# A hybrid encoder step on one core: the order of the first stage, the identity, the PSUM banks of the long projections, and the rank of attention

## The chip, the cores and the metric

The kernel is one program on one core of a Trainium2 chip. It is written in a language in which the author names every instruction and its engine. A scheduler at compile time then fixes the order in which each engine works its instructions off, and puts in the semaphores. The metric is the device time of one execution in microseconds (us). Two executions of the same program differ a little, so a time is given as the median of several runs.

The engines are TensorE (PE, matrix products, with a separate row PEld for the loading of weights), VectorE (DVE), ScalarE (ACT), GpSimd (POOL) and SyncE (SP), whose only work here is to issue transfers.

## The reference

One layer of a streaming encoder works on 384 tokens: 256 of a new stream and 8 running streams of 16 tokens each. All data are float32. With D = 2048:

```python
h    = rmsnorm(x, norm_mix_g)
proj = h @ w_in            # columns: GLU in (2048), q, k, v (1024 each), forget logits (8), gates A and B (2048 each)
u    = glu_in[..., :1024] * sigmoid(glu_in[..., 1024:])
z    = layernorm(causal_dwconv(ext(u), conv_dw_w, conv_dw_b))        # 31 taps
a    = (z * sigmoid(z)) @ conv_pw_out
q, k = rmsnorm(q), rmsnorm(k)
b    = forgetting_attention(q, k, v, logf, caches) @ w_att_out        # 8 heads of 128
x    = x + (sigmoid(gA) * a + sigmoid(gB) * b) @ w_out
h2   = rmsnorm(x, norm_ffn_g)
g, v = split(h2 @ w_up)                                               # 5632 each
x    = x + (silu(causal_dwconv(ext(g), ffn_dw_w, ffn_dw_b)) * v) @ w_down   # 3 taps
```

Beside x the new keys, values, log forget gates and convolution states are returned.

## The kernel before

**Products in three passes.** Each float32 operand of a large product is split into a high part `hi`, in the engine's rounded format, and a low part `lo`, the rest. A product is then three matmuls: hi·hi, lo·hi and hi·lo. Weights come from memory as a stream of tiles `raw`, one per pair of 128-row blocks. The list `plan` holds all 480 pairs in the order of their use. `fetch` (L132) issues the load on SP, `split` (L148) makes `hi` by a copy on ACT (L145) and `lo` by a subtraction on DVE (L146). There are three buffers each for `raw`, `hi` and `lo`. `ahead(n)` (L199) keeps two or three pairs split in advance; its loads and splits carry a priority raised by `SPLIT_AHEAD` = 150.

**Rows of work.** `gemm` (L221) walks a list of jobs. A job of kind "B" has the 384 tokens as three row tiles of up to 512 columns, so it holds three PSUM banks; a job of kind "A" (only the GLU columns) holds four. After each block of 128 rows (a unit: 9 matmuls for "B", 12 for "A") `tick` (L212) advances the side work, which is written as generators: `first_norm`, `bias_rows`, `attention`, `conv`, `layer_norm`. At the end of a job its `evac` takes the banks off to SBUF under a priority raised by `EVAC_AHEAD` = 400. PSUM has eight banks: five in the pool `acc` for the jobs, three in the pool `misc` for transposes and small products.

**What sets the order.** All of PE's instructions run in the order of the source (`pe_order`, L291). On the other engines the scheduler picks, of the instructions that its model calls ready, the one of the best rank. Three devices restrict it. The very first block (L293 to L321) is in source order on SP, ACT and DVE. `queued(d)` (L91) ties an instruction behind the last one queued on its engine. `keep_in_program_order` ties an instruction behind the one traced before it on its engine. Neither adds a wait: they only fix the order, and an engine works strictly along it.

**The first stage.** The columns of v are made first, in three jobs of 344 columns; the first two share one walk over the rows, and the weight tiles of the two alternate. During this walk `first_norm` brings in the input: `x_chunk(c)` (L282) transposes three token tiles by PE into a `misc` bank (L285), and ACT and DVE write the parts of `hT` from it (L288, L289). ACT also sums squares of x (L399), and after the last chunk `rsqrt` gives the row factors `rs1` with which v is scaled when it leaves PSUM (`tok_evac`, L423). The loads of the first sixteen weight pairs are chained on SP with the loads of x; their splits, the `x_chunk` evacuations and the other ACT and DVE work are not chained. The identity for the transposes is made by a helper on POOL (a memset and a select); eight small loads follow on POOL (L348 to L352).

**Keys and queries.** `tok_evac` is called with the index `sq` for k and q. For each of the three banks it writes the rows and then, still inside the raised priority, sums the squares of four heads on ACT (L433).

**Attention and convolution** run beside the GLU jobs. `attention` (L651) starts one head every six units, in six steps: `head_past_keys` (the cached keys transposed on DVE, L571, and the load of the next head's cached keys, L574), `head_operands`, `head_scores`, `head_probs`, `head_out`, `head_last`. All of it has the ordinary rank. `conv` (L686) does 31 taps for each of eight channel groups on DVE (L722) at the ordinary rank, and goes on into the gate jobs.

**After it** come the gate jobs (L823), the two projections of a and b (`AO_PW`, L178) with the mixing, `w_out`, and the feed-forward part (`FFN_PLAN`, L170), all of kind "B" with 512 columns.

Of the kernel before, what the change touches and what calls it, by code (L numbers as in the profile page):

```python
# [15 lines left out]
P = 128  # L16
# [17 lines left out]
SPLIT_AHEAD, EVAC_AHEAD = 150, 400  # L34
# [6 lines left out]
def hybrid_step(  # L41
# [102 lines left out]
    def split_rows(hi, lo, raw, o, k):  # L144
        nc.scalar.copy(hi[:, k, :o], raw[:, k, :o])  # L145
        tt(lo[:, k, :o], raw[:, k, :o], f(hi[:, k, :o]), op=ALU.subtract)  # L146
# [44 lines left out]
    v_last = len(plan) - 16  # L191
    ready = []
# [89 lines left out]
    def x_chunk(c):  # L282
        ps = misc_tile()
        for t in range(NTT):
            tr(ps[:, t * P:(t + 1) * P], xs[c // 4][:, t, c % 4 * P:(c % 4 + 1) * P], ident[:])  # L285
        g = gm[:, c:c + 1]
        hi, lo = hT[c // 4][:, 0, c % 4, :], hT[c // 4][:, 1, c % 4, :]
        nc.scalar.activation(hi, ps[:, :NT], AF.Identity, scale=g)  # L288
        stt(lo, ps[:, :NT], g, f(hi), op0=ALU.mult, op1=ALU.subtract)  # L289
# [57 lines left out]
    for v, r, n in rows:  # L347
        nc.gpsimd.dma_start(vrow[r:r + n, :], v[0].rearrange("(c p) -> c p", p=P))  # L348
    kg = p_qkv.tile([P, P], F32, name="kg")
    nc.gpsimd.dma_start(kg[:], k_norm_g[0].partition_broadcast(P))  # L350
    bf = p_qkv.tile([P, H], F32, name="bf")
    nc.gpsimd.dma_start(bf[:], b_forget[0].partition_broadcast(P))  # L352
# [35 lines left out]
    def first_norm():  # L388
        for c in range(2, 16, 2):
            if c == 2:  # L390
                yield
            yield
            x_chunk(c)
            yield
            x_chunk(c + 1)
            if c % 4 == 2:
                for t in range(NTT):
                    n = c // 4
                    tc.keep_in_program_order(  # L399
                        nc.scalar.activation(junk[:], xs[n][:, t, :], AF.Square, accum_out=ssx[:, t, n:n + 1]))  # L400
            yield
            if c > 2:
                yield
        mt = p_x0.tile([P, NTT], F32, name="mt")
        nc.vector.tensor_reduce(mt[:], ssx[:], axis=mybir.AxisListType.X, op=ALU.add)
        ts(mt[:], mt[:], 1.0 / DM, EPS, op0=ALU.mult, op1=ALU.add)
        r = rsqrt(mt[:], [P, NTT], p_x0, "r1")
        nc.vector.tensor_copy(rs1[:], r[:])
        for _ in range(12):
# [13 lines left out]
    def tok_evac(dst, c0, n, sq=None, shared=True):  # L423
        def ev(t, ps):
            if shared and t % 2:
                ts(dst[:, t, c0:c0 + n], ps[:, :n], rs1[:, t:t + 1], None, op0=ALU.mult)
            else:
                nc.scalar.activation(dst[:, t, c0:c0 + n], ps[:, :n], AF.Identity, scale=rs1[:, t:t + 1])
            if sq is not None:
                for i in range(n // P):  # L430
                    jk = p_qkv.tile([P, P], F32, tag="jk", bufs=2, name="jk")
                    h = c0 // P + i
                    nc.scalar.activation(jk[:], dst[:, t, h * P:(h + 1) * P], AF.Square,  # L433
                                         accum_out=ssq[:, sq, t, h:h + 1])
        return ev
# [78 lines left out]
    gemm([job("B", 16, ha, tok_evac(kt, 512 * i, 512, 0)) for i in range(2)], [bias_rows()])  # L514
# [9 lines left out]
    gemm([job("B", 16, ha, tok_evac(qt, 512 * i, 512, 1)) for i in range(2)])  # L524
# [44 lines left out]
    def head_past_keys(d):  # L569
# [3 lines left out]
        if d["h"] + 1 < H:  # L573
            load_k(d["h"] + 1)  # L574
# [76 lines left out]
    def attention():  # L651
# [171 lines left out]
    gemm([job("B", 16, ha, sig_evac(sg, n)) for sg in (sgA, sgB) for n in range(4)], [ln_steps])  # L823
# [10 lines left out]
    gemm([ao_job(n) for _, n in AO_PW[:2]], [ln_steps])  # L834
# [30 lines left out]
    def pw_done(n):  # L865
        def done():
# [8 lines left out]
          for what, n in AO_PW[2:]])  # L875
# [56 lines left out]
    gemm([job("B", 16, grouped(mix), wo_evac(n), done=wo_done(n)) for n in range(4)])  # L932
# [93 lines left out]
    for what, g in FFN_PLAN:  # L1026
        gemm(up_jobs(g) if what == "up" else down_jobs(g, g[-1] == 10))
# [45 lines left out]
```

## Time and profile before

| | us |
|---|---|
| median of 3 runs | 2005.14 (2003.96 to 2006.22) |
| the profiled execution, time | 2005.83 |
| its span, first to last instruction | 2003.9 |
| PE busy (9431 matmuls) | 1992.6 |
| PEld busy | 1681.5 |
| DVE busy | 1272.2 |
| ACT busy | 742.1 |
| POOL busy | 87.2 |
| mean granted PE clock | 0.999 |

The page of the profile gives, for each engine, the time in which it worked on something and its share of the span. Idle time of an engine has a cause: a wait for a semaphore, which the view of the waits names by the instruction that released it. A matmul's recorded length overlaps that of the next, so the distance from start to start tells its cost. The clock that the throttle granted to PE is a share of full speed. The memory moved 137 GB/s on average over the span.

### The profile page before, as it was taken

Reading aid. Unit: us, or ns where it says so; the run is one execution under the profiler, and the core shown is the slowest. Engines: PE = TensorE matmul, PEld = TensorE weight load, DVE = VectorE, ACT = ScalarE, POOL = GpSimd, SP = SyncE. Lnnn points to the kernel's source line nnn. Section 1 sums busy time; section 2 is a strip of 40 time slices with the busy share of each in tenths; the row PEclk is TensorE's granted clock in tenths of the full one; section 3 lists DMA queues with packets and bytes.
Section 4 is the critical chain, followed back from the end, with each engine's and each line's share of the span. In section 5 each row is a group of like instructions: output and inputs, shape, how many; then the busy total and the mean of one; then the engine's idle time right before and its main releaser. Section 6 shows DMA issues by size and latency. Waiting matters only on the chain.

```text
span 2003.9 us, 24493 instructions
## 1 busy us (share of the span) xinstructions
PE 1992.6 (99%) x9431; PEld 1681.5 (84%) x9431; DVE 1272.2 (63%) x1852; ACT 742.1 (37%) x1077; POOL 87.2 (4%) x216
## 2 busy tenths in 40 slices
PE   8999999999999999999999999999999999999999
PEld 8988999988888887888888888888888888888887
DVE  4435478888765487676867683367673376638663
ACT  5434455433334523334433432233332233323321
POOL 2000001100000000000010000001000000000000
PEclk9999999999999999999999999999999999999999
DMA  6566566444444334534444444444443444344443
GB/s 179 176 175 175 137 163 167 120 140 131 132 134 125 127 121 142 185 121 133 127 137 116 137 127 137 126 127 126 129 135 127 133 120 137 126 129 125 137 157 106
DMA packets 209254, 275.99 MB, mean 138 GB/s; under 512 B 55878, under 2 KB 96729, under 8 KB 209129
## 3 DMA queue, kind: packets, MB, share of 16 engines
q1 hardware_dynamic: 208817, 273.85, 46.3%
q8 instruction: 74, 1.21, 0.2%
q0 software_dynamic: 288, 0.57, 0.2%
q14 instruction: 43, 0.35, 0.1%
q10 hardware_dynamic: 32, 0.01, 0.0%
HBM read 266.98 MB, written 7.86 MB: 137 GB/s over the span
## 4 chain that ended last, share of the span: by engine, by line
PE 95%; DVE 4%; issue 1%; DMA 1%; ACT 0%; SPq 0%; ACTq 0%; DVEq 0%
PE acc L244 28%; PE acc L246 28%; PE acc L245 28%; PE acc L239 2%; PE acc L241 2%; PE acc L240 2%; DVE mixT L259 1%; DVE lo L146 1%; DMA raw<-in_w_in_dram 1%; DVE sgA L843 0%; DVE uT L259 0%; DVE sgA L844 0%; PE misc L636 0%; PE misc L603 0%; PE misc L285 0%
## 5 line engine op out<-in xcount | busy, mean ns | idle before, releaser
L146 DVE TENSOR_TENSOR lo<-raw,hi 128x1024 fp32r<-128x1024 f32 (+2 forms) x481 | 579.6, 1205 | 582.7 <-ACT hi L145 579.0
L145 ACT CAST hi<-raw 128x1024 fp32r<-128x1024 f32 (+2 forms) x481 | 496.0, 1032 | 994.2 <-PE acc L246 869.1
L244 PE MATMUL acc<-hi,xg 128*128 128x512 f32 x1056 | 411.8, 390 | 0.0
L246 PE MATMUL acc<-hi,xg 128*128 128x512 f32 x1056 | 410.9, 389 | 0.0
L245 PE MATMUL acc<-lo,xg 128*128 128x512 f32 x1056 | 410.8, 389 | 0.0
L244 PE MATMUL acc<-hi,hT 128*128 128x512 f32 (+1 forms) x704 | 268.5, 381 | 2.4 <-ACT hT L288 2.4
L246 PE MATMUL acc<-hi,hT 128*128 128x512 f32 (+1 forms) x704 | 266.0, 378 | 0.4 <-DVE hT L289 0.4
L245 PE MATMUL acc<-lo,hT 128*128 128x512 f32 (+1 forms) x704 | 265.8, 377 | 0.0
L244 PEld LDWEIGHTS acc<-hi,xg 128*128 128x128 f32 x1056 | 198.2, 188 | 42.3
L246 PEld LDWEIGHTS acc<-hi,xg 128*128 128x128 f32 x1056 | 198.2, 188 | 41.3
L245 PEld LDWEIGHTS acc<-lo,xg 128*128 128x128 f32 x1056 | 198.2, 188 | 40.6
L244 PE MATMUL acc<-hi,act 128*128 128x512 f32 x528 | 205.5, 389 | 0.5 <-DVE y L1018 0.5
L246 PE MATMUL acc<-hi,act 128*128 128x512 f32 x528 | 205.4, 389 | 0.0
L245 PE MATMUL acc<-lo,act 128*128 128x512 f32 x528 | 205.4, 389 | 0.0
L722 DVE SCALAR_TENSOR_TENSOR ut<-ext,cw,ut 128x384 f32<-128x384 f32 x240 | 151.5, 631 | 6.1
L244 PEld LDWEIGHTS acc<-hi,hT 128*128 128x128 f32 x704 | 132.7, 189 | 25.3 <-ACT hT L288 2.7
L246 PEld LDWEIGHTS acc<-hi,hT 128*128 128x128 f32 x704 | 132.7, 189 | 23.3 <-DVE hT L289 0.7
L245 PEld LDWEIGHTS acc<-lo,hT 128*128 128x128 f32 x704 | 132.8, 189 | 22.2
L259 DVE STREAM_TRANSPOSE extf<-tok 32x384 f32<-32x384 f32 x176 | 100.3, 570 | 30.9 <-ACT tok L954 28.2
L259 DVE STREAM_TRANSPOSE uT<-tok 32x384 f32<-32x384 f32 x176 | 100.3, 570 | 29.7 <-ACT tok L954 26.9
L244 PEld LDWEIGHTS acc<-hi,act 128*128 128x128 f32 x528 | 99.1, 188 | 21.6 <-DVE y L1018 0.9
L245 PEld LDWEIGHTS acc<-lo,act 128*128 128x128 f32 x528 | 99.1, 188 | 20.5
(289 smaller groups left out, 2079.7 us busy)
## 6 DMA issues: line engine op xcount, KB each, us to landing
raw<-in_w_up_dram SPq DMA_DIRECT2D x176, 512.0 KB
raw<-in_w_in_dram SPq DMA_DIRECT2D x96, 512.0 KB
raw<-in_w_down_dram SPq DMA_DIRECT2D x88, 512.0 KB
raw<-in_w_in_dram SPq DMA_DIRECT2D x64, 256.0 KB
raw<-in_w_out_dram SPq DMA_DIRECT2D x32, 512.0 KB
raw<-in_w_att_out_dram SPq DMA_DIRECT2D x16, 512.0 KB
raw<-in_conv_pw_out_dram SPq DMA_DIRECT2D x16, 512.0 KB
raw<-in_w_in_dram SPq DMA_DIRECT2D x23, 344.0 KB
```

Of the source, the lines that this page charges most:

```text
L145: nc.scalar.copy(hi[:, k, :o], raw[:, k, :o])
L146: tt(lo[:, k, :o], raw[:, k, :o], f(hi[:, k, :o]), op=ALU.subtract)
L239: mm(o, hi[:, kk, s], ah, start=st, stop=False)
L240: mm(o, hi[:, kk, s], al, start=False, stop=False)
L241: mm(o, lo[:, kk, s], ah, start=False, stop=sp)
L244: mm(o, ah[:, s], hi[:, kk, :n], start=st, stop=False)
L245: mm(o, ah[:, s], lo[:, kk, :n], start=False, stop=False)
L246: mm(o, al[:, s], hi[:, kk, :n], start=False, stop=sp)
L259: nc.vector.transpose(put(a, slice(32 * b, 32 * b + 32)), src[32 * a:32 * a + 32, b])
L722: stt(o, v, wc, o, op0=ALU.mult, op1=ALU.add)
```

## The change

Five things are changed together.

1. **The first stage is chained.** `queued` now also covers the splits on ACT and DVE of the first twenty weight pairs (`in_first()`), the two evacuations of each `x_chunk` (which also get `EVAC_AHEAD`), the last squares of x, the square root of `rsqrt`, and the ACT evacuations of the first two v jobs. So ACT and DVE do these in the order of the source. The reduction that leads to `rs1` is raised in rank and comes two units earlier in the walk; the waits after it are two units longer, so the rest of `first_norm` stays where it was.
2. **The identity** is made by two POOL instructions written out and queued first; the eight small POOL loads are queued behind them.
3. **`wide`**: in the gate jobs, the projections, `w_out` and the feed-forward part, a job takes two banks from `acc` and its third from `misc`. The v, k, q and GLU jobs stay as they were.
4. **Squares of k and q** move out of the evacuation into `post`, behind all three banks of the job and at the ordinary rank.
5. **Attention's steps** are traced under a priority raised by `ATT_AHEAD` = 250. The load of the next head's cached keys moves out of `head_past_keys` and is issued right after the step, at the ordinary rank.

```diff
-SPLIT_AHEAD, EVAC_AHEAD = 150, 400
+SPLIT_AHEAD, ATT_AHEAD, EVAC_AHEAD = 150, 250, 400
-    make_identity(nc, ident[:])
+    nc.gpsimd.memset(ident[:], 0.0)
+    queued(nc.gpsimd.affine_select(out=ident[:], in_=ident[:], pattern=[[-1, P]], compare_op=ALU.not_equal, fill=1.0,
+                                   base=0, channel_multiplier=1))
-        nc.scalar.activation(s, m, AF.Sqrt)
+        queued(nc.scalar.activation(s, m, AF.Sqrt), in_first())
     def split_rows(hi, lo, raw, o, k):
-        nc.scalar.copy(hi[:, k, :o], raw[:, k, :o])
-        tt(lo[:, k, :o], raw[:, k, :o], f(hi[:, k, :o]), op=ALU.subtract)
+        first = in_first()
+        queued(nc.scalar.copy(hi[:, k, :o], raw[:, k, :o]), first)
+        queued(tt(lo[:, k, :o], raw[:, k, :o], f(hi[:, k, :o]), op=ALU.subtract), first)
+    def in_first():
+        return len(plan) >= v_last - 4
-    def gemm(jobs, sides=()):
+    def gemm(jobs, sides=(), wide=False):
-                j["ps"] = [(misc_tile if j is not js[0] and i == 2 else acc_tile)() for i in range(nb)]
+                j["ps"] = [(misc_tile if i == 2 and (wide or j is not js[0]) else acc_tile)() for i in range(nb)]
+                    if "post" in j:
+                        j["post"]()
-        nc.scalar.activation(hi, ps[:, :NT], AF.Identity, scale=g)
-        stt(lo, ps[:, :NT], g, f(hi), op0=ALU.mult, op1=ALU.subtract)
+        with tc.high_priority(offset=EVAC_AHEAD):
+            queued(nc.scalar.activation(hi, ps[:, :NT], AF.Identity, scale=g))
+            queued(stt(lo, ps[:, :NT], g, f(hi), op0=ALU.mult, op1=ALU.subtract))
-        nc.gpsimd.dma_start(vrow[r:r + n, :], v[0].rearrange("(c p) -> c p", p=P))
+        queued(nc.gpsimd.dma_start(vrow[r:r + n, :], v[0].rearrange("(c p) -> c p", p=P)))
...
-                    tc.keep_in_program_order(
-                        nc.scalar.activation(junk[:], xs[n][:, t, :], AF.Square, accum_out=ssx[:, t, n:n + 1]))
-            yield
-            if c > 2:
+                    sq = nc.scalar.activation(junk[:], xs[n][:, t, :], AF.Square, accum_out=ssx[:, t, n:n + 1])
+                    if c == 14:
+                        queued(sq)
+                    else:
+                        tc.keep_in_program_order(sq)
+            if c < 14:
+                yield
+            if 2 < c < 14:
                 yield
...
+    def tok_job(dst, c0, n, sq):
+        d = job("B", 16, ha, tok_evac(dst, c0, n))
+
+        def post():
+            for t in range(NTT):
+                for h in range(c0 // P, (c0 + n) // P):
+                    jk = p_qkv.tile([P, P], F32, tag="jk", bufs=2, name="jk")
+                    nc.scalar.activation(jk[:], dst[:, t, h * P:(h + 1) * P], AF.Square,
+                                         accum_out=ssq[:, sq, t, h:h + 1])
+        d["post"] = post
+        return d
...
-        if d["h"] + 1 < H:
-            load_k(d["h"] + 1)
...
-                step(d)
+                with tc.high_priority(offset=ATT_AHEAD):
+                    step(d)
+                if step is head_past_keys and d["h"] + 1 < H:
+                    load_k(d["h"] + 1)
...
-    gemm([job("B", 16, ha, sig_evac(sg, n)) for sg in (sgA, sgB) for n in range(4)], [ln_steps])
+    gemm([job("B", 16, ha, sig_evac(sg, n)) for sg in (sgA, sgB) for n in range(4)], [ln_steps], wide=True)
...
-        gemm(up_jobs(g) if what == "up" else down_jobs(g, g[-1] == 10))
+        gemm(up_jobs(g) if what == "up" else down_jobs(g, g[-1] == 10), wide=True)
```

More of the change, by code (lines that the diff above doesn't have):

```diff
@@ L427, in ev @@
             else:
[L428 to L434, printed above, removed]
+                queued(nc.scalar.activation(dst[:, t, c0:c0 + n], ps[:, :n], AF.Identity, scale=rs1[:, t:t + 1]),
+                       in_first())
         return ev
@@ L512, in head_rsqrt @@
         return rsqrt(ssf, [P, NTT * H], p_qkv, f"rq{a}")[:].rearrange("p (t h) -> p t h", t=NTT)
-    gemm([job("B", 16, ha, tok_evac(kt, 512 * i, 512, 0)) for i in range(2)], [bias_rows()])
+    gemm([tok_job(kt, 512 * i, 512, 0) for i in range(2)], [bias_rows()])
     close_b()
@@ L522, in hybrid_step @@
     nc.sync.dma_start(sample_k[0].rearrange("b t h d -> (b t) (h d)"), kt[:, 2, :])
-    gemm([job("B", 16, ha, tok_evac(qt, 512 * i, 512, 1)) for i in range(2)])
+    gemm([tok_job(qt, 512 * i, 512, 1) for i in range(2)])
     rq = head_rsqrt(1)
@@ L874, in hybrid_step @@
     gemm([ao_job(n) if what == "ao" else job("B", 8, grouped(zt), pw_evac(n), done=pw_done(n))
-          for what, n in AO_PW[2:]])
+          for what, n in AO_PW[2:]], wide=True)
     res = {}
@@ L930, in second_norm @@
         nc.vector.tensor_copy(rs2[:], r2[:])
-    gemm([job("B", 16, grouped(mix), wo_evac(n), done=wo_done(n)) for n in range(4)])
+    gemm([job("B", 16, grouped(mix), wo_evac(n), done=wo_done(n)) for n in range(4)], wide=True)
     p_f, y, xg, rs2, close_f, close_r = (res[k] for k in ("f", "y", "xg", "rs2", "close_f", "close_r"))
```

19 lines of the change are left out of this document (10 added, 9 removed).

## The prediction

> **What bounds the kernel now.** I read four views in this order: the page's busy times, PE's waits, the stretches around the largest wait, and the timeline there. First the page.
>
> ```profile
> PE 1992.6 (99%) x9431; PEld 1681.5 (84%) x9431; DVE 1272.2 (63%) x1852; ACT 742.1 (37%) x1077; POOL 87.2 (4%) x216
> ```
>
> PE works in 1992.6 of the span's 2003.9 us, so no reordering of other engines can win more than 11.3 us (0.6%). What PE waited for, in us (total, times, longest):
>
> ```profile
> PE misc L308 <- POOL ident masks.py:199: 2.5, 1, 2.5
> PE acc L244 <- ACT hT L288: 2.4, 1, 2.4
> PE acc L244 <- DVE y L1018: 0.5, 1, 0.5
> PE acc L246 <- DVE hT L289: 0.4, 1, 0.4
> PE acc L244 <- DVE sgB L828: 0.4, 2, 0.2
> PE misc L850 <- DVE sgA L844: 0.2, 1, 0.2
> PE acc L244 <- DVE sgA L843: 0.2, 1, 0.2
> ```
>
> The wait for the identity is at the very start. The second and fourth rows belong together, at 14 to 17 us. The others are waits for PSUM banks or for mixed data. No row comes from the attention stage. The end of the program costs the rest:
>
> ```profile
> 1998.01 2.05 DVE L1018 TENSOR_TENSOR y<-acc,y 128x512 f32<-128x512 f32 x3 [8.57 <-PE acc L246]
> ```
>
> These last three additions follow PE's last matmuls and feed the last stores; no edit touches that. Three stretches of one length, with PE's busy time and its clock (the share after POOL's busy time):
>
> ```profile
> 14.04:17.45 3.41, 0.84 (x3) 0.56 (x4) 2.20 (x4) 2.51 (x5) 0.00 (x0) 1.00 0.73 229
> 17.45:20.88 3.43, 3.43 (x14) 3.43 (x13) 1.00 (x2) 1.93 (x6) 0.00 (x0) 0.50 0.89 266
> 20.88:24.31 3.43, 3.43 (x25) 3.39 (x25) 1.46 (x3) 1.83 (x3) 0.00 (x0) 1.00 0.22 61
> ```
>
> The idle stretch is followed by one at half clock. So the stall is paid twice.
>
> **The first stage chained.** The timeline of the stall (start, length; in brackets idle time before and what ended it):
>
> ```profile
> 5.30 0.43 SPq L137 DMA_DIRECT2D raw<-in_w_in_dram  x1
> 11.56 0.49 PE L285 MATMUL misc<-ident,xs 128*128 128x128 f32 x3
> 12.85 0.77 ACT L145 CAST hi<-raw 128x688 fp32r<-128x688 f32 x1 [3.96 <-DMA raw<-in_w_in_dram]
> 13.30 0.49 PE L285 MATMUL misc<-ident,xs 128*128 128x128 f32 x3
> 13.65 0.87 DVE L146 TENSOR_TENSOR lo<-raw,hi 128x688 fp32r<-128x688 f32 x1 [3.76 <-ACT hi L145]
> 14.94 0.77 ACT L145 CAST hi<-raw 128x688 fp32r<-128x688 f32 x1 [1.32 <-DMA raw<-in_w_in_dram]
> 15.61 0.57 ACT L288 ACTIVATE hT<-misc,gm 128x384 fp32r<-128x384 f32 x1
> 15.73 0.88 DVE L146 TENSOR_TENSOR lo<-raw,hi 128x688 fp32r<-128x688 f32 x1 [1.21 <-ACT hi L145]
> 16.23 0.43 PE L244 MATMUL acc<-hi,hT 128*128 128x344 f32 x1 [2.44 <-ACT hT L288]
> 16.53 0.61 DVE L289 SCALAR_TENSOR_TENSOR hT<-misc,gm,hT 128x384 fp32r<-128x384 f32 x1
> 17.19 0.45 PE L246 MATMUL acc<-hi,hT 128*128 128x344 f32 x1 [0.38 <-DVE hT L289]
> 17.45 0.48 PE L244 MATMUL acc<-hi,hT 128*128 128x344 f32 x1
> 20.88 0.33 PE L244 MATMUL acc<-hi,hT 128*128 128x344 f32 x1
> 24.87 0.32 PE L244 MATMUL acc<-hi,hT 128*128 128x344 f32 x1
> 27.55 0.33 PE L246 MATMUL acc<-hi,hT 128*128 128x344 f32 x1
> ```
>
> Chunk 2 of x was transposed at 11.56. ACT then waited for the third weight pair (issued at 5.30, here at 12.85), made its `hi`, and waited again for the fourth (14.94) before it came to chunk 2 at 15.61. In the source the fourth split stands behind `x_chunk(2)` and `x_chunk(3)`, since `ahead` reaches it two units later. Chained, ACT goes from the third split to chunk 2: the two casts' step to the next instruction is 15.61 − 14.94 = 0.67, so chunk 2 starts at 13.52, ends at 14.09, and PE starts 0.05 later (16.23 against 15.61 + 0.57), at 14.14. On DVE the step from a `lo` to the next is 16.53 − 15.73 = 0.80: chunk 2's `lo` starts at 13.65 + 0.80 = 14.45, ends at 15.06, and the third matmul starts at 15.11 instead of 17.19. **Gain 2.08 us.** What is left, 13.8 to 15.1, is the third load: the split stands ahead of chunk 2 in the source too, so a load on time would be needed for more.
>
> What is queued behind the chain's waits: the fourth split now follows chunk 3 on ACT (about 14.5) and still meets its load at 14.94; its `lo` is done near 16.6 and PE needs it two units later, near 17.9. The fifth split is tied behind chunk 4. A unit of nine matmuls takes 9 × 0.158 = 1.42 (below), so chunk 4 is transposed near 17.8; its activation takes till 18.4, the split's `lo` starts 0.80 later (13.65 − 12.85) and ends near 20.1. PE needs it two units and a transposition later, near 20.9. This is the thinnest cover, 0.8 us by these steps. The raw buffer of the fifth pair comes free some 2 us later than at present, and the eighth load with it; it is wanted only at 27. The square root and the v evacuations in the chain stand where the source needs them.
>
> **Half clock.** Between 17.45 and 20.88 lie twelve matmuls (0.286 each); from 24.87 to 27.55 there are seventeen steps (0.158 each). With PE idle for about 0.8 us after 14.04 (15.11 − 14.04, less two matmuls), instead of 3.41 − 0.84 = 2.57, I expect no half clock: 12 × 0.128 = **1.54 us**. The bounds are 0 and 1.54; 2.6 of 3.41 us busy is nearer to the stretch with 3.43, which ran on at full clock, than to the one with 0.84, so I take 1.54.
>
> [...]
>
> **Identity first.** The POOL rows, and what PE needs next:
>
> ```profile
> 0.81 0.20 POOL masks.py:197 MEMSET ident<- 128x128 f32 x1 [0.29 <-POOLq L1060]
> 1.39 0.68 POOL L348 DMA_DIRECT2D vrow<-in_norm_ffn_g_dram  x1 [0.37 <-issue]
> 2.15 0.32 POOL masks.py:199 TENSOR_SCALAR_AFFINE_SELECT ident<-ident 128x128 f32<-128x128 f32 x1
> 8.92 0.97 DVE L146 TENSOR_TENSOR lo<-raw,hi 128x688 fp32r<-128x688 f32 x1
> 10.29 0.32 PE L245 MATMUL acc<-lo,hT 128*128 128x344 f32 x1
> ```
>
> The select moves ahead of one small load, so the identity is ready about 1 us sooner and the warm-up matmuls start sooner. It is worth nothing: the second pair's `lo` (8.92 + 0.97 = 9.89) leaves only 0.4 us to its use at 10.29, and behind it the third load bounds all. PE would merely wait longer there. The eight POOL loads slide by a fraction of a microsecond and no row shows anyone waiting for them.
>
> **Eight banks.** The rows of one of the bank waits:
>
> ```profile
> 721.42 0.68 DVE L828 TENSOR_TENSOR sgB<-acc,sgB 128x512 f32<-128x512 f32 x1
> 721.59 0.39 PE L246 MATMUL acc<-hi,zt 128*128 128x512 f32 x1
> 722.16 0.50 PE L244 MATMUL acc<-hi,zt 128*128 128x512 f32 x1 [0.18 <-DVE sgB L828]
> ```
>
> A job of three banks out of five meets, at its third tile, the job just ended, whose first bank DVE was still emptying. With two from `acc` and one from `misc` a new job takes banks of the job before the last. Start to start the loss is 0.57 less 0.23 = 0.35; three such waits (`sgB` twice, `sgA`) make 1.04, and the one for `y` costs its 0.48 and the same 0.16 of refilling: **1.7 us**. Bounds: 0, if DVE itself is what is late, and 1.7; I take 1.7 because the banks of a whole job are then spare. The price is on `misc`: at a job's border two of its three banks are held, and side transposes share the third. They come at least a unit apart, so I put it at nothing; without that cover each would wait one evacuation, the 0.68 us above.
>
> **Squares of k and q** cost no instruction more. They run later on ACT, behind splits. What needs them is the scaling of q, then PE:
>
> ```profile
> 229.90 1.22 DVE L528 TENSOR_TENSOR qt<-qt,rq1r 128x1024 f32<-128x1024 f32 x1
> 235.13 0.49 PE L583 MATMUL misc<-ident,qt 128*128 128x128 f32 x3
> ```
>
> Scaling ends at 231.12, 4.0 us ahead of the first transposition. One or two casts slipped in between (0.77 each above for 688 columns) fit. Cost nothing.
>
> **Attention's rank.** Same instructions; attention now goes ahead of splits where both are ready. No PE wait can be removed, since there is none. What is at stake:
>
> ```profile
> 356.92 1.23 DVE L571 STREAM_TRANSPOSE kTs<-kc 128x1024 f32<-128x1024 f32 x1
> 358.54 3.50 DVE L146 TENSOR_TENSOR lo<-raw,hi 128x1024 fp32r<-128x1024 f32 x3 [0.21 <-ACT hi L145]
> 360.82 0.34 PE L240 MATMUL acc<-hT,hi 128*128 128x384 f32 x1
> ```
>
> For the last head the keys were transposed late, and the first of three splits that piled up behind it ended near 359.7, about 1 us before PE came to its pair at 360.54. With the higher rank this transposition can be done as soon as the head before has used its buffer, well before the splits. Value: between a loss of 1.23 per head and a small relief; I take nothing. The loads of the keys stay where the source has them on SP, so SP's queue does not change its order around weights.
>
> **The sum.** 2005.83 − 2.08 − 1.54 − 1.7 = 2000.5. The profiled execution lies 0.7 above the median of 2005.14, so against that median it is −0.23%. About 0.2%, 4 us, is what a measurement of this kernel can tell from no change; the forecast is just past it.
>
> **The rivals.**
>
> *The clock's dip does not change sides* (0.17). Executions before may lack it, or those after may still have it, since about 1 us of stall is left at the third load. Then 1.54 is not won: 2002.0, no difference that can be told. For it speaks that the executions before spread by 2.3 us, more than one dip; against it that only the stretch with 0.84 us of work is followed by a dip in these rows.
>
> *The loads bound the first stage anyway* (0.12). If the third and fourth pairs or chunk 4 land later once the order moves, or the fifth split is late by more than its 0.8 us, PE stops two units further on and the first stage gives nothing. Only the banks remain: 2005.83 − 1.7 = 2004.1. For it speaks the DMA share of 0.73 and 0.89 (the last column but one) in the first two stretches; against it the 0.22 from 20.88 on, when the loads had caught up.
>
> *Attention in front of the splits stops PE* (0.18). DVE takes its instructions in one order, so a key transposition that stands ahead of a split and waits for a load, or merely runs, holds the split back. If each of the eight heads costs one uncovered 1.23 us, that is 9.8: 2000.5 + 9.8 = 2010.3, slower. It decides from the point where a split is held back past its cover, about 1 us at 358.54; against it speaks that this is the thinnest place and comes from a transposition that ran late, which the rank cures.
> [...]
>
> **How the numbers follow.** The forecast has 0.53, in its own range of 1999.0 to 2001.3. Its lower end adds what else PE waits for near the mixing (0.2), the 0.4 of the second pair, and 0.7 between the profiled run and the median; its upper end leaves half of the bank term unwon. With the two rivals that end short of a change (2002.0 and 2004.1) 0.82 is held by 1999.0 to 2005.0. Faster 0.53, same 0.17 + 0.12 = 0.29, slower 0.18.
>
> **What would show it.** Chunk 2's activation directly behind the third cast, PE's wait at 14 us cut to about 1 us in all, and clock 1.00 after it; the identity at 1.3 us with a longer wait later; no wait of L244 for `sgB`, `sgA` or `y`; no PE wait between 235 and 385. It would be wrong if PE shows new waits for `hi` or `lo` there, if the wait at the third pair grows, or if a dip of the clock remains.

## The result, and the profile after

The changed kernel takes 2007.95 us (median) where the kernel before takes 2005.14 in the same series: a ratio of 1.0016, with a 95% interval of 1.0009 to 1.0023. The prediction put what can be told from no change at about 0.2%; this lies within that, a shade on the slow side, with the whole interval above 1. The forecast was 2000.5. Two executions of the changed kernel, of 2857.61 us here and of 10643.46 us in a later series, ran slow and are left out of the ratios. The profiled execution took 2008.16 us with a span of 2006.3, against 2005.83 and 2003.9 before.

The page's busy times of the changed kernel:

```profile
PE 1994.2 (99%) x9431; PEld 1683.3 (84%) x9431; DVE 1273.5 (63%) x1852; ACT 742.9 (37%) x1077; POOL 85.9 (4%) x216
```

The counts are those of before, and PE again fills 99%. The view of PE's waits (total, times, longest) shows that the kernel is another one all the same. This is the whole list:

```profile
PE misc L651 <- DVE mx L628: 5.0, 2, 3.5
PE misc L317 <- POOL ident L109: 1.5, 1, 1.5
PE misc L872 <- DVE sgA L866: 0.5, 2, 0.3
PE misc L343 <- DVE ln L337: 0.2, 1, 0.2
```

The waits for `hT`, `sgB` and `y` are gone, as forecast. At the top stands a wait that did not exist: L651, the first matmul of `head_out`, waits twice for L628, the reduction over the scores in `head_scores`.

To see what each stretch of the program gained or lost, take the first and the last GLU matmul. Attention runs beside the GLU jobs, so these two times cut the span into the part up to the keys and queries, the attention stage, and the rest. In the view of one line's instructions (count, shortest/median/longest ns, first and last start in us), before:

```profile
L239 PE MATMUL acc<-hT,hi x256: 333/334/443, 218.5 to 389.5; 128*128 128x384 f32 x128
```

and after, where the same line is L245:

```profile
L245 PE MATMUL acc<-hT,hi x256: 333/334/667, 214.2 to 393.6; 128*128 128x384 f32 x128
```

| | up to the GLU jobs | attention stage | rest of the span |
|---|---|---|---|
| before | 218.5 | 389.5 − 218.5 = 171.0 | 2003.9 − 389.5 = 1614.4 |
| after | 214.2 | 393.6 − 214.2 = 179.4 | 2006.3 − 393.6 = 1612.7 |
| difference | −4.3 | +8.4 | −1.7 |

So the gains came, 6.0 us of them, and the attention stage took 8.4 back. The longest GLU matmul went from 443 to 667 ns: a sign of half clock in that stage (it starts at 367.05, inside the stretches at 0.50 shown below).

**Where the 8.4 us went.** The timeline of the changed kernel around the two stops (start, length; in brackets idle time before and what ended it):

```profile
336.56 0.42 SPq L579 DMA_DIRECT2D bs<-c_dr  x1
341.79 0.72 POOL L584 TENSOR_TENSOR bs<-bs,mk 128x256 f32<-128x256 f32 x1 [24.21 <-DMA bs<-c_dr]
342.55 0.29 DVE L628 CUSTOM_DVE_ANT_0 pr<-misc,bs 128x128 f32<-128x128 f32 x1 [1.30 <-POOL bs L584]
342.90 0.49 PE L651 MATMUL misc<-vt,pT 128*128 128x128 f32 x2 [1.47 <-DVE mx L628]
343.88 11.89 SPq L139 DMA_DIRECT2D raw<-in_w_in_dram  x6
355.87 0.41 SPq L576 DMA_DIRECT2D vc<-in_cache_v_dram  x1
356.96 0.63 SPq L579 DMA_DIRECT2D bs<-c_dr  x1
362.90 0.72 POOL L584 TENSOR_TENSOR bs<-bs,mk 128x256 f32<-128x256 f32 x1 [5.53 <-DMA bs<-c_dr]
363.66 0.29 DVE L628 CUSTOM_DVE_ANT_0 pr<-misc,bs 128x128 f32<-128x128 f32 x1 [4.59 <-DMA sc<-in_state_conv_dram]
364.01 0.79 PE L651 MATMUL misc<-vt,pT 128*128 128x128 f32 x2 [3.50 <-DVE mx L628]
```

Read it from the bottom. PE stands 3.50 us at L651, which needs nothing of the last head's scores but a bank of `misc`; all three banks of that pool hold the scores until DVE reduces them. DVE reduces them as soon as POOL has added the mask to `bs` (363.66 follows 362.90 + 0.72; the name in the bracket of that row is that of a transfer which merely ended near it). POOL waits for `bs` to land, and `bs` was issued late: SP had spent 11.89 us on six weight loads (two to each pair of these columns), 7.8 of them in one wait until DVE's split had freed a `raw` buffer, and `vc` and `bs` of the last head stood behind them. One head earlier the same chain cost 1.47. In the kernel before, the same `bs` load left SP 9.4 us sooner, POOL's addition did not wait for it, and the reduction came 14.4 us after the issue:

```profile
347.58 0.43 SPq L558 DMA_DIRECT2D bs<-c_dr  x1
356.98 0.74 POOL L563 TENSOR_TENSOR bs<-bs,mk 128x256 f32<-128x256 f32 x1
361.95 0.29 DVE L609 CUSTOM_DVE_ANT_0 pr<-misc,bs 128x128 f32<-128x128 f32 x1
```

What the second stop did to the clock, in stretches of 3.41 us (PE's busy time comes first, the clock after POOL's):

```profile
359.62:363.03 3.41, 0.90 (x6) 0.58 (x4) 0.00 (x0) 0.00 (x0) 0.13 (x1) 1.00 0.81 241
363.03:366.44 3.41, 2.43 (x21) 1.79 (x22) 1.75 (x12) 1.25 (x5) 1.05 (x2) 0.50 0.27 59
366.44:369.86 3.42, 3.42 (x14) 3.42 (x14) 0.84 (x3) 1.64 (x5) 0.00 (x0) 0.50 0.07 11
369.86:373.27 3.41, 3.41 (x22) 3.38 (x21) 1.52 (x2) 1.47 (x2) 0.00 (x0) 1.00 0.10 16
```

PE worked from 364.01 to 369.86, 5.85 us, at a clock of 0.50, and that, with the refilling behind the stop, cost 2.9 us: from the GLU matmul that starts at 358.16 to the one at 369.98 lie 11.82 us, where the same two lie 5.42 apart in the kernel before (360.54 and 365.96), and 3.50 of the 6.40 between them are the stop. The sum: 1.47 + 3.50 + 2.9 = 7.9 of the 8.4; the rest is the refilling behind the first stop (across it the GLU matmuls slip by 1.74 against before, of which 1.47 are the stop), a slip of 0.14 at the last head's scores, and rounding.

**The first stage** of the changed kernel, in its timeline:

```profile
12.23 0.77 ACT L148 CAST hi<-raw 128x688 fp32r<-128x688 f32 x1 [3.62 <-DMA raw<-in_w_in_dram]
12.91 0.58 ACT L297 ACTIVATE hT<-misc,gm 128x384 fp32r<-128x384 f32 x1
13.64 0.40 PE L250 MATMUL acc<-hi,hT 128*128 128x344 f32 x1
14.40 0.76 ACT L148 CAST hi<-raw 128x688 fp32r<-128x688 f32 x1
14.49 0.43 PE L252 MATMUL acc<-hi,hT 128*128 128x344 f32 x1
```

Chunk 2's activation follows the third cast directly, the fourth cast comes two activations later, and PE starts chunk 2 at 13.64 without a wait. The third matmul of chunk 2 starts at 14.49, where 15.11 was forecast. The 0.62 between them is the third weight load, whose cast stands at 12.23 instead of 12.85 although the load left SP at the same time (5.31, before 5.30).

### The profile page after: what moved, and what is told of

It reads as the page before. It is cut to its first block, busy times and chain, and to the rows that moved or that the text cites. A ratio compares the mean times of both kernels' runs of the same rounds, so it can differ in the third digit from the quotient of the medians.

```text
span 2006.3 us, 24486 instructions
## 1 busy us (share of the span) xinstructions
PE 1994.2 (99%) x9431; PEld 1683.3 (84%) x9431; DVE 1273.5 (63%) x1852; ACT 742.9 (37%) x1077; POOL 85.9 (4%) x216
## 4 chain that ended last, share of the span: by engine, by line
PE 96%; DVE 2%; DMA 1%; SPq 0%; issue 0%; ACT 0%; POOL 0%; POOLq 0%; ACTq 0%; DVEq 0%
PE acc L250 21%; PE acc L252 21%; PE acc L251 21%; PE misc L252 9%; PE misc L250 9%; PE misc L251 9%; PE acc L245 2%; PE acc L246 2%; PE acc L247 2%; DVE lo L149 1%; DVE mixT L267 0%; DMA raw<-in_w_in_dram 0%; DMA vc<-in_cache_v_dram 0%; DMA bs<-c_dr 0%; PE misc L655 0%
## 5 line engine op out<-in xcount | busy, mean ns | idle before, releaser
L250 PE MATMUL acc<-hi,xg 128*128 128x512 f32 x704 | 274.9, 390 | 0.0
L252 PE MATMUL acc<-hi,xg 128*128 128x512 f32 x704 | 273.9, 389 | 0.0
L251 PE MATMUL acc<-lo,xg 128*128 128x512 f32 x704 | 273.9, 389 | 0.0
L250 PE MATMUL acc<-hi,hT 128*128 128x512 f32 (+1 forms) x576 | 218.3, 379 | 0.0
L252 PE MATMUL acc<-hi,hT 128*128 128x512 f32 (+1 forms) x576 | 215.8, 375 | 0.1
L251 PE MATMUL acc<-lo,hT 128*128 128x512 f32 (+1 forms) x576 | 215.8, 375 | 0.0
L250 PEld LDWEIGHTS acc<-hi,xg 128*128 128x128 f32 x704 | 132.1, 188 | 28.3
L252 PEld LDWEIGHTS acc<-hi,xg 128*128 128x128 f32 x704 | 132.1, 188 | 27.5
L251 PEld LDWEIGHTS acc<-lo,xg 128*128 128x128 f32 x704 | 132.2, 188 | 27.1
L252 PE MATMUL misc<-hi,xg 128*128 128x512 f32 x352 | 137.0, 389 | 0.0
L250 PE MATMUL misc<-hi,xg 128*128 128x512 f32 x352 | 137.0, 389 | 0.0
L251 PE MATMUL misc<-lo,xg 128*128 128x512 f32 x352 | 136.9, 389 | 0.0
L250 PE MATMUL acc<-hi,act 128*128 128x512 f32 x352 | 136.9, 389 | 0.0
L251 PE MATMUL acc<-lo,act 128*128 128x512 f32 x352 | 136.9, 389 | 0.0
L252 PE MATMUL acc<-hi,act 128*128 128x512 f32 x352 | 136.9, 389 | 0.0
```

The source lines that it names most:

```text
L250: mm(o, ah[:, s], hi[:, kk, :n], start=st, stop=False)
L251: mm(o, ah[:, s], lo[:, kk, :n], start=False, stop=False)
L252: mm(o, al[:, s], hi[:, kk, :n], start=False, stop=sp)
```

## The experiments

The theory after the result: the raised rank of attention changed the order in which the compiled program issues loads on SP, and the late `bs` made the two stops; nothing else in the change costs anything. The rivals: the earlier first stage, the squares or the banks make the stops; or attention ahead of the splits costs by itself. The order on SP is fixed at compile time, so it can be counted: how many weight loads stand ahead of a load in SP's list. Two of them make a pair in this stage, and a range means that weight loads stand between the four parts of a load.

| weight loads ahead of | before, and without the rank | changed; rank alone | loads raised by 120 | loads raised by 70 | late loads |
|---|---|---|---|---|---|
| `bs`, head 5 | 103 | 103 to 105 | 99 | 103 | 107 |
| `bs`, head 6 | 109 | 113 | 105 | 109 | 113 |
| `bs`, head 7 | 115 | 119 | 111 | 115 | 115 |
| `kc`, head 7 | 109 | 113 | 105 | 109 | 109 to 110 |

All runs beside the kernel before on the same chip:

| kernel | median, us | before, us | ratio (95%) | stop of PE in the attention stage |
|---|---|---|---|---|
| attention at the ordinary rank | 2000.00 | 2004.13 | 0.9979 (0.9970 to 0.9988) | none |
| rank alone | 2012.32 | 2004.13 | 1.0040 (1.0028 to 1.0053) | 2 at L630 |
| first stage and identity alone | 2001.74 | 2004.13 | 0.9988 (0.9980 to 0.9997) | none |
| rank, loads raised by 120 | 2007.67 | 2004.13 | 1.0017 (1.0008 to 1.0026) | 1 at a weight pair (5.2), 0.3 behind it |
| late loads, no rank | 2018.20 | 2004.83 | 1.0069 (1.0056 to 1.0082) | 4 at L651 |
| rank, loads raised by 70 | 2000.25 | 2004.83 | 0.9978 (0.9969 to 0.9987) | none |
| eight banks alone | 2002.02 | 2004.83 | 0.9991 (0.9982 to 1.0000) | none |
| ordinary rank, identity by the helper | 1999.88 | 2004.83 | 0.9976 (0.9967 to 0.9986) | none |
| squares alone | 2005.07 | 2005.26 | 0.9998 (0.9989 to 1.0007) | none |
| before again | 2005.50 | 2005.26 | 1.0000 (0.9991 to 1.0009) | none |
| changed again | 2008.56 | 2005.26 | 1.0016 (1.0007 to 1.0026) | 2 at L651 |

### Attention at the ordinary rank

```diff
-                with tc.high_priority(offset=ATT_AHEAD):
-                    step(d)
+                step(d)
```

> The changed kernel with attention's steps back at the ordinary rank, all else as changed. Theory (the raised rank made the compiled order put the loads of vc and bs for heads 6 and 7 behind weight loads that wait for a buffer; PE then stood for 1.6 and 3.7 us and ran 6.8 us at half clock): no wait of PE at L651 in the attention stage, clock 1.00 there, about 2008.0 - 8.7 = 1999.3, at most 2001. Rival (the stops come from the first stage being 4 us earlier, from the squares moved behind the evacuation, or from the eight banks): the stops at 341 and 360 us stay and the time is 2007 to 2008.

2000.00 us, ratio 0.9979 (0.9970 to 0.9988). The row of the GLU line:

```profile
L245 PE MATMUL acc<-hT,hi x256: 333/335/444, 214.4 to 385.5; 128*128 128x384 f32 x128
```

The last head's load and addition in the timeline:

```profile
343.56 0.42 SPq L579 DMA_DIRECT2D bs<-c_dr  x1
...
352.83 0.74 POOL L584 TENSOR_TENSOR bs<-bs,mk 128x256 f32<-128x256 f32 x1
```

And one of PE's waits:

```profile
PE acc L250 <- ACT hT L297: 1.3, 1, 1.3
```

The attention stage is back at 385.5 − 214.4 = 171.1. The wait is in the first stage, for chunk 1 of x (at 9 us). The load leaves 9.3 us before the addition, which again waits for nothing. All of the loss came with the rank, and the other four edits together win 0.2% and land on the forecast; how much of that is luck is said below.

### The rank alone

```diff
-SPLIT_AHEAD, EVAC_AHEAD = 150, 400
+SPLIT_AHEAD, ATT_AHEAD, EVAC_AHEAD = 150, 250, 400
...
-        if d["h"] + 1 < H:
-            load_k(d["h"] + 1)
...
-                step(d)
+                with tc.high_priority(offset=ATT_AHEAD):
+                    step(d)
+                if step is head_past_keys and d["h"] + 1 < H:
+                    load_k(d["h"] + 1)
```

> The kernel before with attention's raised rank alone (the load of the next head's keys moved out of the raised part, as in the change). Theory: the two stops of PE at L651 appear without any of the other edits, with or without half clock behind them: 2005.1 + 1.6 + 3.7 = 2010.4, to 2013.8 with a half clock of 3.4 us. Rival (the rank is harmless by itself, only the earlier first stage brings the loads out of step): 2005, no wait at L651.

2012.32 us, 1.0040 (1.0028 to 1.0053). PE's longest wait, where L630 is `head_out` and L607 the reduction:

```profile
PE misc L630 <- DVE mx L607: 4.5, 2, 3.3
```

The row of the GLU line:

```profile
L239 PE MATMUL acc<-hT,hi x256: 333/335/667, 216.0 to 393.9; 128*128 128x384 f32 x128
```

The two stops (3.3 and 1.2) are there without any of the other edits, and the stage takes 177.9. The rival that needs the earlier first stage has fallen.

### The first stage and the identity alone

The kernel before with parts 1 and 2 of the change, and with none of the others:

```diff
-    make_identity(nc, ident[:])
+    nc.gpsimd.memset(ident[:], 0.0)
+    queued(nc.gpsimd.affine_select(out=ident[:], in_=ident[:], pattern=[[-1, P]], compare_op=ALU.not_equal, fill=1.0,
+                                   base=0, channel_multiplier=1))
...
+    first = in_first()
+    queued(nc.scalar.copy(hi[:, k, :o], raw[:, k, :o]), first)
+    queued(tt(lo[:, k, :o], raw[:, k, :o], f(hi[:, k, :o]), op=ALU.subtract), first)
...
```

> The kernel before with the chained first stage and the identity alone. Theory: the gain of 4.26 us at the first GLU matmul is kept to the end: 2005.1 - 4.3 = 2000.8; by the prediction's own two terms 2005.1 - 2.08 - 1.54 = 2001.5. Rival (what the first stage wins is lost later because loads bound what follows): 2004 to 2005.

2001.74 us, 0.9988 (0.9980 to 0.9997). The row of the GLU line:

```profile
L245 PE MATMUL acc<-hT,hi x256: 333/335/444, 213.6 to 384.7; 128*128 128x384 f32 x128
```

The first stage is 4.9 earlier than in the profile before, and the stage after it has 171.1: nothing is given back. Against the 2004.13 on that chip the gain is 2.4 us (0.6 to 4.0 by the interval), which holds both the 3.6 of the prediction's two terms and the 2.1 of the first alone; so this run does not tell whether the half clock was won in the median.

### Attention's rank with its loads raised by 120

```diff
                 if step is head_past_keys and d["h"] + 1 < H:
-                    load_k(d["h"] + 1)
+                    with tc.high_priority(offset=120):
+                        load_k(d["h"] + 1)
                 if step is head_out and d["h"] + 2 < H:
-                    load_v(d["h"] + 2)
+                    with tc.high_priority(offset=120):
+                        load_v(d["h"] + 2)
```

> The changed kernel, attention's rank raised as changed, but the loads of vc, bs and kc are raised too, by 120 (below the weights' 150). In the compiled order of SP the bs loads of heads 5, 6 and 7 then stand behind 99, 105 and 111 weight loads instead of 103 to 105, 113 and 119 (before: 103, 109, 115). Theory (the place of the loads is the cause, not what attention's rank does on DVE, ACT or PE): no wait at L651, 1999.3 to 2001. Rival (attention in front of the splits costs by itself): PE still stops and the time is 2004 or more.

2007.67 us, 1.0017 (1.0008 to 1.0026): a miss. The stops at L651 are gone, as the theory said, but another has come. PE's longest wait:

```profile
PE acc L245 <- ACT hi L148: 5.2, 1, 5.2
```

The timeline ahead of it:

```profile
345.52 3.03 DVE L746 SCALAR_TENSOR_TENSOR ut<-ext,cw,ut 128x384 f32<-128x384 f32 x3
348.58 0.39 ACT L728 COPY ext<-ut 128x240 f32<-128x240 f32 x1 [3.25 <-DVE ut L746]
349.14 2.94 ACT L148 CAST hi<-raw 128x1024 fp32r<-128x1024 f32 x3
350.23 0.69 PE L245 MATMUL acc<-hT,hi 128*128 128x384 f32 x1 [5.22 <-ACT hi L148]
```

ACT's order had changed as well. The cast of the next weight pair now stood behind two copies for the convolution, which waited 3.25 us for taps on DVE. This is the loss that the prediction's third rival described, a split held back in a queue worked off in order, though by the convolution and not by a key transposition. By itself this run does not tell whether the rank or the loads' rank made it; a later one does.

### Late loads without the rank

```diff
-                    load_v(d["h"] + 2)
+                    with tc.high_priority(offset=-100):
+                        load_v(d["h"] + 2)
```

> The kernel of the first experiment (attention at the ordinary rank) with the vc and bs loads of heads 2 to 7 lowered by 100 in rank. In the compiled order of SP the bs loads of head 6 then stand behind 113 weight loads, as in the changed kernel (109 before), those of heads 2 to 5 behind 85, 95, 101 and 107 (79, 87, 95 and 103 before), those of head 7 behind 115 as before. Theory (the place of the bs loads alone makes the stops): PE stops at L651 with attention's rank untouched, at head 6 by about 1.5 us and at the earlier heads whose loads moved by four or more places; with 1 to 4 such stops and half clocks 2001.5 to 2012. Rival (only the raised rank makes the stops): 2000, no wait at L651.

2018.20 us, 1.0069 (1.0056 to 1.0082). PE's longest wait:

```profile
PE misc L651 <- DVE mx L628: 12.8, 4, 5.4
```

Two of its four stops in the timeline:

```profile
290.30 0.49 PE L651 MATMUL misc<-vt,pT 128*128 128x128 f32 x2 [0.45 <-DVE mx L628]
...
313.10 0.80 PE L651 MATMUL misc<-vt,pT 128*128 128x128 f32 x2 [5.33 <-DVE mx L628]
```

The row of the GLU line:

```profile
L245 PE MATMUL acc<-hT,hi x256: 333/334/667, 214.4 to 403.4; 128*128 128x384 f32 x128
```

Loads issued late make the stops with attention at its ordinary rank: head 6, whose `bs` stands as in the changed kernel, costs 1.6 us (1.47 there); heads 4 and 5 cost 5.3 and 5.4, with half clock at each (0.50 from 313.10 to 318.30, a mean of 0.69 from 334.00 to 337.40), and a fourth stop 0.45. The cause is shown from both sides. The time, 2018.20, lies above the 2012 that I had allowed, a miss in size: I had not counted stops of over 5 us.

### Attention's rank with its loads raised by 70

The same edit as with 120, with 70 in both places, which brings `vc`, `bs` and `kc` of heads 5 to 7 back to the places of before (the last part of head 5's `kc` alone stands one load later).

> The changed kernel with attention's rank at 250 as changed, and its loads raised by 70, which puts the vc, bs and kc loads of heads 5 to 7 behind as many weight loads as with the ordinary rank (bs 103, 109, 115). Theory (with its loads where they were, the rank costs nothing and wins nothing): no stop at L651 and none at a weight pair, 1999.5 to 2001. Rival (attention ahead of the splits on DVE and ACT costs by itself): 2002 or more, with waits for hi or lo between 235 and 385 us.

2000.25 us, 0.9978 (0.9969 to 0.9987). The row of the GLU line:

```profile
L245 PE MATMUL acc<-hT,hi x256: 333/334/443, 214.2 to 385.2; 128*128 128x384 f32 x128
```

The last head's load and addition in the timeline:

```profile
343.65 0.59 SPq L579 DMA_DIRECT2D bs<-c_dr  x1
...
352.56 0.74 POOL L584 TENSOR_TENSOR bs<-bs,mk 128x256 f32<-128x256 f32 x1
```

The stage takes 171.0. With the loads where they were, the rank costs nothing and wins nothing against the 2000.00 without it. So the rank does no harm by itself on DVE, ACT or PE, and the stop with 120 came with the loads' rank of 120. Whether 120 would bring it without attention's rank was not run.

### Eight banks alone

The kernel before with part 3 of the change:

```diff
-                j["ps"] = [(misc_tile if j is not js[0] and i == 2 else acc_tile)() for i in range(nb)]
+                j["ps"] = [(misc_tile if i == 2 and (wide or j is not js[0]) else acc_tile)() for i in range(nb)]
...
```

> The kernel before with two banks of acc and one of misc for the long projections alone. Theory: the four bank waits go, 2005.1 - 1.7 = 2003.4 (the first and third experiment differ by 1.74, with the squares in it). Rival (the held misc banks make the mixing or the side work wait by as much): 2005.

2002.02 us, 0.9991 (0.9982 to 1.0000). Of PE's waits from the gate jobs on, one is left:

```profile
PE misc L850 <- DVE sgA L844: 0.5, 2, 0.3
```

The rows for `sgB`, `sgA` at L843 and `y` are gone; the wait of the mixing has grown from 0.2 to 0.5. The row of the GLU line:

```profile
L239 PE MATMUL acc<-hT,hi x256: 333/334/443, 216.4 to 387.5; 128*128 128x384 f32 x128
```

From the last GLU matmul (387.5) to the end of the span (1999.9) it takes 1612.4, against 1614.4 before: 2.0 less. The medians differ by 2.8, which is 1.4 below the forecast, but the ratio, 0.9991, is 1.8 us with an interval from nothing to 3.6. The predicted 1.7 fits the ratio and the profiles; of the executions with a mean clock of 1.000 alone, the medians are 2001.80 and 2003.24, 1.4 apart (for these groups see the half clock below).

### The identity by the helper again

```diff
-    nc.gpsimd.memset(ident[:], 0.0)
-    queued(nc.gpsimd.affine_select(out=ident[:], in_=ident[:], pattern=[[-1, P]], compare_op=ALU.not_equal, fill=1.0,
-                                   base=0, channel_multiplier=1))
+    make_identity(nc, ident[:])
```

> The kernel of the first experiment with the identity made by the helper again, as before, not queued first. Theory, as predicted: the identity's place is worth nothing, 2000.0. Rival (the first microsecond at PE's start carries through): 2000.5 to 2001.

1999.88 us, 0.9976 (0.9967 to 0.9986), beside 0.9979 with the identity first. PE waits 2.5 us for the identity instead of 1.5 and nothing changes.

### Squares alone, before again, changed again

The first is the kernel before with part 4 of the change; the others have no edit.

```diff
+                    if "post" in j:
+                        j["post"]()
...
-    gemm([job("B", 16, ha, tok_evac(kt, 512 * i, 512, 0)) for i in range(2)], [bias_rows()])
+    gemm([tok_job(kt, 512 * i, 512, 0) for i in range(2)], [bias_rows()])
...
```

> The kernel before with the squares of k and q moved behind the evacuation alone. Theory, as predicted: worth nothing, 2005 within 1 us; its first stage is that of before, so the wait for chunk 2 at 14 to 17 us is seen once more, 1.4 to 2.4 us, with or without half clock. Rival (the squares behind splits delay the scaling of q and the first transposition of attention): a wait of PE near 230 us, 2006 or more; or (banks come free sooner) 2004 or less.

> The kernel before once more, for its first stage. If the half clock behind the stop of 2.4 us belongs to every execution: the same stop, then 3.4 us at 0.50, a span of 2003 to 2004. If it depends on the size of the stop, which the arrival of the third and fourth weight pairs sets: a stop of 1.4 to 1.5 us as in the second and seventh experiment, clock 1.00 behind it, a span of 2001 to 2002.

> The changed kernel once more, for the two stops at L651. Theory (they are set by the compiled order of SP): both stops again, 1.5 and 3.5 us within 0.5 us each, and half clock behind the second for 3.4 or 6.8 us; 2006 to 2009. Rival (they come from the chance arrival of loads): stops of other sizes or at other heads, or none.

The squares: 2005.07 us, 0.9998 (0.9989 to 1.0007), worth nothing as predicted. Its first stage is that of before, and so is that of the kernel before run again; the two show what the stop at 14 us can be. Stretches of 3.41 us with the squares alone:

```profile
12.59:16.00 3.41, 1.00 (x8) 0.74 (x6) 1.06 (x2) 1.75 (x3) 0.00 (x0) 1.00 0.91 303
16.00:19.41 3.41, 3.09 (x9) 2.65 (x10) 2.52 (x4) 3.35 (x9) 0.00 (x0) 0.50 0.78 221
19.41:22.83 3.42, 3.42 (x14) 3.36 (x14) 0.00 (x0) 0.68 (x3) 0.00 (x0) 0.50 0.65 204
```

The wait for chunk 2 in the kernel before, run again:

```profile
PE acc L244 <- ACT hT L288: 1.6, 1, 1.6
```

Its stretches:

```profile
11.30:14.71 3.41, 2.82 (x20) 2.54 (x18) 0.88 (x1) 1.03 (x2) 0.00 (x0) 1.00 1.02 351
14.71:18.12 3.41, 2.00 (x11) 1.72 (x12) 2.71 (x4) 3.38 (x8) 0.00 (x0) 1.00 0.67 173
18.12:21.54 3.42, 3.42 (x25) 3.39 (x24) 1.22 (x2) 2.05 (x5) 0.00 (x0) 1.00 0.82 276
```

The execution with the squares stopped for 2.7 us, more than the 2.4 allowed, and paid two stretches of half clock; that of before stopped for 1.6, with 2.82 and 2.00 us of work in the two stretches around it, and paid none. Its span was 2001.8, while other executions of the same kernel take some 2 us more. The half clock does not belong to every execution of the kernel before. The third cast, which waits for its load, stood at 12.98 with the squares, at 12.85 in the profile before and at 12.42 here: the later the load, the longer the stop (2.7, 2.4 and 1.6 us).

The changed kernel again, 2008.56 us, and its longest wait:

```profile
PE misc L651 <- DVE mx L628: 4.4, 2, 3.2
```

The same two stops at the same heads (1.2 and 3.2 us): they belong to the program, not to chance.

## Why the prediction was wrong

**The step that failed** is the last sentence on attention's rank: "The loads of the keys stay where the source has them on SP, so SP's queue does not change its order around weights", and with it "I take nothing". A load at the ordinary rank is not tied to its place. The scheduler chose anew: `kc` of head 7 came to stand behind 113 weight loads instead of 109, and `bs`, the load that stopped PE and that the prediction does not name, behind 119 instead of 115. Four weight loads are two pairs; a pair waits for a `raw` buffer, and SP, which works its list off in order, issued `vc` and `bs` (355.87 and 356.96) only behind the six that it began at 343.88, with its wait of 7.8 us among them. What attention's rank cost was 8.4 us where the sum had 0: 5.0 of stops, 2.9 of half clock, and refilling. I had weighed the rank on DVE alone (1.23 per head) and never asked how much time the loads of a head have. Before, `bs` of the last head left SP 14.4 us ahead of the reduction that uses it (347.58 to 361.95). In the changed kernel it left 3.55 us before PE came to L651 (356.96 to 360.51), and landing, addition and reduction took 7.05 (to 364.01): the difference is the stop of 3.50. The sign I named, "no PE wait between 235 and 385", is the one that failed. Why the scheduler moved the loads is not settled: the order follows from its model, which no trace shows. What is shown is that the rank alone moves them.

**The rivals.** "Attention in front of the splits stops PE" has the right stage and nearly the size (8.4 against 9.8), but not the mechanism: no row of the changed kernel shows PE waiting for `hi` or `lo` there, and with the load order restored the rank costs nothing. "The clock's dip does not change sides" was partly right about the kernel before: its dip comes in some executions only. In the profile of the changed kernel the clock reads 1.00 from 9 to 363.03 us, and in three others with the first stage chained (first stage and identity alone, loads raised by 70, identity by the helper) its mean of 1.000 leaves no room for a stretch of 3.41 at half clock behind the very start; for the other four no view covers the first stage in full. "The loads bound the first stage anyway" did not hold.

**The first stage chained (2.08) and the half clock (1.54).** The mechanism is right: the order on ACT is as forecast, and the stop and the dip are gone. In the size there is luck. The 4.3 between the two profiles has 0.6 of a third load that landed sooner, which no edit brought, and the whole dip of the profiled execution, from which the sum starts. Not every execution pays that dip. Beside the first four experiments, 13 of the 27 executions of the kernel before have a mean clock of 0.999 (median 2005.17 us) and 14 one of 1.000 (2003.44). The 1.73 between them is half of a stretch of 3.41, and the two profiles of that kernel, with the dip (0.999) and without (1.000), differ likewise (spans of 2003.9 and 2001.8); that each of the 13 had the dip is not shown. So, if they had it, the 1.54 is won in about half of the executions on that chip, and the medians give 2.4 for both terms (0.6 to 4.0). The stop that I left at the third load was none in this profile; with attention at the ordinary rank one of 1.3 us remained at chunk 1, one chunk earlier than I had it, and the changed kernel run again had two, of 0.5 and 0.3.

**Eight banks (1.7).** Right: 1.7 from the last GLU matmul to the end in the changed kernel. Alone it gives 2.0 between the profiles and 1.8 in the ratio. I had priced the held `misc` banks at nothing; the mixing's wait grew by 0.3.

**Identity and squares (0 and 0).** Right, each by its own run.

Without the rank, the sum's other terms came out: 2000.00 measured, 2000.5 forecast. Such closeness has luck in it, since the sum starts from an execution 0.7 above the median and takes a whole dip off it. The range has a slip too: the three amounts named for its lower end lead to 1999.2, not 1999.0. The three fastest kernels are the changed kernel with attention at the ordinary rank, with or without the helper's identity, and the one with the rank and its loads raised by 70. They do not differ from one another within what these runs can tell.

## What to carry to other kernels

When a change raises the rank of some work, list every queue that the scheduler orders, the queue that issues transfers first of all, and compare the order before and after: a rank moves things that were not touched (here `bs` of the last head, from behind 115 weight loads to behind 119). A load with a few microseconds of slack (here 3.55, where 7.05 were needed) must not stand behind loads that wait for a buffer; ask of each load how long it has from issue to use, and tie its place down if that is short. And when PE waits for a bank, ask who holds the banks: here the waiting matmul needed nothing of the late data.

## What the runs showed of the hardware

**Half clock lasted 3.4 us or twice that, and a stretch need not be idle to be followed by it.** The clock stood at 0.50 for 3.43 us before (17.45 to 20.88), for 3.41 with the rank alone (365.84 to 369.25), and for 6.83 both in the changed kernel (363.03 to 369.86) and with the squares alone (16.00 to 22.83). In the 3.41 us just ahead of these falls PE was busy for 0.84 us (before), 0.45 (rank alone), 0.90 (changed) and 1.00 (squares alone). Stretches of that length with 1.79 us of work (late loads, 356.07 to 359.50), 2.00 and 2.82 (before again) and 2.30 (changed, 339.13 to 342.55), around stops of 1.47 to 1.6 us, were followed by full clock. The way back is stricter in these rows: stretches at half clock with 3.41 us of work (rank alone), 3.42 (the second of the changed kernel and of the squares alone) and 3.43 (before) were followed by full clock, but with 2.43 (changed) and 3.09 (squares alone) the next stretch stayed at half. Behind the very start, each stop of 2.4 us or more whose clock a view shows (2.44, 2.7, 3.3, 3.50, 5.2, 5.3) was paid a second time and none of 1.6 or less. The second price was 1.5 us before (twelve steps of 0.286, where a step at full clock takes 0.158) and 2.9 in the changed kernel; with the squares alone it is 3.3 by an estimate, half of the 3.09 + 3.42 us worked at 0.50. So what was followed by half clock goes up to 1.00 us of work in 3.41, and what was followed by full clock begins at 1.79; what holds between them, and whether the place of a stop counts beside its length, these rows do not tell.

**A stop of one engine can be four queues long.** `bs` was late on SP, so POOL, DVE and PE stopped in turn. The load itself was hardly slower: between the issue at 356.96 and POOL's start at 362.90 lay 5.9 us for 128 KB, and for the seven heads whose addition waited for the same load in the kernel before, it was 4.2 to 5.4. What had moved was the place in SP's queue.
